# The end of the last expert in another order: a decoder trunk on one core

## The chip, the cores and the metric

The kernel runs on one core of a Trainium2 chip. The metric is the device time of one execution in microseconds (us); the runs shown are three executions. The engines are called by the names of the profile: PE is TensorE (matrix products), PEld its weight loads, DVE is VectorE, ACT is ScalarE, POOL is GpSimd, SP is SyncE, which here issues all transfers.

## The reference, cut to what matters

Two decoder layers over 256 tokens of width 1024. The part around the change is the end of the second layer: eight experts, each token sent to two of them, then a layer norm, then a gate with the input embedding.

```python
def moe(x, w_r, w1, w3, w2):                       # x: 256 tokens x 1024
    ...
    for e in range(N_EXPERTS):                     # 8 experts, inner width 3584
        out = out + combine[:, e:e + 1] * swiglu(xt, w1[e], w3[e], w2[e])

f = moe(x, ...)
x = layer_norm(DN_ALPHA * x + f, ln2_g[i], ln2_b[i])
gate = jax.nn.sigmoid(x @ ple_w_g[i] + ple_b_g[i])  # 1024 x 1024 weight
x = x + gate * (p[i] @ ple_w_p[i])
```

## The kernel before

The 256 tokens are two blocks of 128 rows (b = 0 and 1). Weights come through one stream of 1 MB loads ("raw" tiles, `Stream.load`, L204) that SP issues in a fixed order, up to eight in flight. The buffers are ten ring tiles and nine "cut" slots which the stream may borrow while the experts run.

Experts (`moe`, L1056): each expert has four steps of columns; a step is an up product (tiles `m`), SiLU and product on ACT and DVE (`mh`), a transposition on PE (`mt`, L1150) and a down product into the tile `py`. Expert weights are used as plain f32. When an expert is done, `rows` (L1161) copies its result out of PSUM as a high part (ACT, L1169) and a rest (DVE, L1170), tile `y`, and `spread` (L1180) multiplies it by the routing matrix on PE (tile `sc`, L1192), once for each block and each half of 512 columns; DVE adds it with its weight to the accumulator `acc` (L1193). For the first seven experts `spread` runs one expert later, between weight loads; for the eighth nothing comes after it.

The end (`finish`, L875, one generator for each block): layer norm of `acc[b]` on DVE (BN_STATS, BN_AGGR, L437 `n_w`, an inverse root on POOL L439 `n_r`, then L520 and L521, two instructions each, into `xn`); eight transpositions on PE (L455, `x2T_t`), whose results ACT and DVE write as a high part and a rest (L443, `x2T`); then `product` (L468): the gate weight comes in four 1 MB loads = eight pieces of 128 rows; each piece is split into a high part by ACT (L159) and a rest, the "second part", by DVE (L161), tile `hl`; a piece costs six matmuls of 512 columns into two PSUM banks `fin` (L462 high x high, L464 x the weight's rest, L466 the rest of x). So a block costs 48 matmuls. The two blocks use the same split pieces; `side_by_side` (L237) lets block 1 follow block 0 by up to six pieces (`LAG_G`). At the product's start the bias goes in as a one-row matmul for each bank (L472). `gated` (L806) does the sigmoid on ACT, two DVE operations and the store of each bank.

Each engine runs its own instructions strictly in the order written in its queue; that order is fixed when the program is built, by a scheduler that takes the program's order and the priorities (`high_priority`), and an instruction that waits holds all behind it on its engine.

Of the kernel before, what the change touches and what calls it, by code (L numbers as in the profile page):

```python
# [15 lines left out]
OP = mybir.AluOpType  # L16
# [51 lines left out]
TAFT = 4  # L68
STEPS = (2, 4)
# [35 lines left out]
class Stream:  # L105
# [3 lines left out]
    def __init__(self, tc, nc, raw, cut):  # L109
        self.tc = tc  # L110
        self.nc, self.rings, self.cut = nc, [raw], cut
        self.idle, self.busy, self.lend, self.lent = list(range(SPL)), {}, 0, []
        self.extra = []
        self.room, self.size = [RAW], [RAW]
        self.units, self.pieces, self.lags, self.stays = [], [], [], set()
        self.left = [None]
# [8 lines left out]
        self.whole, self.held = set(), {}  # L125
# [11 lines left out]
    def _split(self, v):  # L137
# [40 lines left out]
    def add_ring(self, pool, n):  # L178
        self.rings.append(pool)
        self.room.append(n)  # L180
        self.size.append(n)
        self.left.append(None)

    def raw_tile(self, name, stays=False, dtype=F32):

        for r in range(len(self.rings)):
            if self.room[r] and self.left[r] != 0:
                self.room[r] -= 1
                if self.left[r] is not None:
                    self.left[r] -= 1  # L190
                elif stays:
                    self.left[r] = self.size[r] - 1
# [56 lines left out]
def trunk(ctx: ExitStack, tc: tile.TileContext, a, out):  # L249
# [57 lines left out]
    for i in range(DEPTH):  # L307
# [15 lines left out]
        else:  # L323
# [144 lines left out]
    def product(b, ps, xT, ks, between=iter(()), bias=None):  # L468

        if bias is not None:  # L470
            for c in range(2):
                nc.tensor.matmul(ps[c], lhsT=one, rhs=bias[:, c * 512:(c + 1) * 512], start=True, stop=False)  # L472
        held = []
        for n, k in enumerate(ks):
# [391 lines left out]
    moe(tc, a, st, x, acc, xtp, rt, early, ident, const, small, ps_mm, ps_tr, ps_s, mm3, split_from)  # L866
    st.alone = False
    st.lend = 0
    late = ctx.enter_context(tc.tile_pool(name="late", bufs=2))
    st.load()  # L870
    row, pbg = st.raws[rows0], st.raws[rows0 + 1]
    rows_bc[f"L{last}g2"], rows_bc[f"L{last}b2"] = row[:, :D], row[:, D:]
    xn = [late.tile([P, D], F32, name=f"xn{b}", bufs=1) for b in range(NB)]

    def finish(b):  # L875

        if b == 0:
            xT = [late.tile([P, KT, P], F32R, name=f"x2T{b}{j}", bufs=1) for j in range(2)]
        else:
            t, _ = st.raw_tile("x2T1", dtype=F32R)  # L880
            xT = [t[:, j * D:(j + 1) * D].rearrange("p (k t) -> p k t", k=KT) for j in range(2)]
        ps = [ps_mm(b, f"fin{b}{c}") for c in range(2)]
# [3 lines left out]
        if b == 0:  # L886
            st.limit = None
            st.after = [normed.ins] * TAFT
        yield from product(b, ps, xT, range(KT), bias=pbg[0:1, :D])
        gated(b, ps, L_[last]["pp"][b], xn[b])  # L890

    side_by_side(st, [finish(b) for b in range(NB)])
# [163 lines left out]
def moe(tc, a, st, x, acc, xtp, rt, early, ident, const, small, ps_mm, ps_tr, ps_s, mm3, split_from):  # L1056
# [5 lines left out]
    with tc.tile_pool(name="moe", bufs=2) as mp:  # L1062
# [98 lines left out]
        def rows(e, py):  # L1161
# [18 lines left out]
        def spread(e, y, plT):  # L1180
# [6 lines left out]
            for b in range(NB):  # L1187
# [20 lines left out]
        for s, (e, c) in enumerate(steps):  # L1208
            hh = up(s, xg)
# [133 lines left out]
```

## Time and profile before

| what | us |
|---|---|
| runs | 1299.16, 1298.37, 1297.72; median 1298.37 |
| the profiled execution, its own time | 1299.9 |
| its span (first to last instruction in the trace) | 1298.0 |
| busy: PE, PEld, DVE, ACT, POOL | 1239.5, 725.6, 424.0, 309.9, 26.7 |
| last expert weight has landed | 1249.95 |
| block 0's transpositions start | 1263.08 |
| block 1's transpositions start | 1277.17 |
| last gate matmul ends | 1290.6 |
| last DVE instruction ends, span ends | 1292.7, 1298.0 |

All times of the trace are counted from the span's start. The profiled execution took 1.9 us more than its span, and 1.5 us more than the median run. A matmul's row shows when it starts and how long it is in the engine; matmuls overlap, so the step from one start to the next is what one costs.

### The profile page before, as it was taken

How to read it: one execution, taken by the hardware profiler on the slowest of the kernel's cores; microseconds unless marked ns; L12 is line 12 of the kernel's file. 1: busy time of each engine (PE TensorE's matmuls, PEld its weight loads, DVE VectorE, ACT ScalarE, POOL GpSimd, SP SyncE). 2: the span in 40 equal slices, each digit the busy share in tenths (PEclk: the TensorE clock that was granted, in tenths of full speed). 3: DMA queues.
4: the chain of work that ended last, by engine and by line, in shares of the span. 5: the costliest groups of instructions: out<-in, count | busy, mean ns of one | idle time of the engine just before them, and what ended most of it. 6: DMA issues, size and time to landing. Idle time of an engine off the chain costs nothing.

```text
span 1298.0 us, 27799 instructions
## 1 busy us (share of the span) xinstructions
PE 1239.5 (95%) x12214; PEld 725.6 (56%) x12214; DVE 424.0 (33%) x772; ACT 309.9 (24%) x505; POOL 26.7 (2%) x71
## 2 busy tenths in 40 slices
PE   8999999999999999999999999999899999978787
PEld 7888888887888556533323555533455543312126
DVE  7868554558876121011010111011012112001035
ACT  6754443445663101010100100010000001000022
POOL 1100000000100000000000000000000000000000
PEclk9999999999999899999999999999999999999988
DMA  9626554656549999999999999999999999999970
GB/s 328 228 65 207 184 177 150 223 188 194 206 143 371 405 364 364 356 421 421 421 420 420 420 420 419 420 421 420 420 420 419 419 420 420 421 421 421 421 287 35
DMA packets 83406, 431.59 MB, mean 333 GB/s; under 512 B 8615, under 2 KB 15309, under 8 KB 40270
## 3 DMA queue, kind: packets, MB, share of 16 engines
q1 hardware_dynamic: 83278, 429.74, 83.5%
q8 instruction: 98, 1.61, 0.5%
q14 instruction: 30, 0.25, 0.1%
HBM read 428.66 MB, written 1.05 MB: 331 GB/s over the span
## 4 chain that ended last, share of the span: by engine, by line
PE 72%; DMA 24%; DVE 2%; ACT 1%; issue 1%; POOL 0%; SPq 0%; ACTq 0%
DMA raw<-in_moe_w 23%; PE m L1110 17%; PE py L1110 8%; PE m L1105 7%; PE ff L462 3%; PE ff L464 3%; PE ff L466 3%; PE py L1105 3%; PE f L466 2%; PE f L462 2%; PE f L464 2%; PE g L988 2%; PE mt L1150 1%; PE sc L1192 1%; PE fin L462 1%; PE fin L464 1%
## 5 line engine op out<-in xcount | busy, mean ns | idle before, releaser
L1105 PE MATMUL m<-raw,xg 128*32 128x512 f32 x2240 | 251.0, 594 | 15.1 <-DMA raw<-in_moe_w 14.4
L1110 PE MATMUL m<-raw,xg 128*32 128x256 f32 x3024 | 225.8, 381 | 2.2 <-DMA raw<-in_moe_w 1.4
L1111 PE MATMUL m<-raw,xg 128*32 128x256 f32 x1008 | 224.0, 381 | 0.0
L1110 PEld LDWEIGHTS m<-raw,xg 128*32 128x32 f32 x3024 | 129.6, 110 | 87.1 <-issue 4.3
L1105 PEld LDWEIGHTS m<-raw,xg 128*32 128x32 f32 x2240 | 68.8, 110 | 185.5 <-issue 140.9
L161 DVE TENSOR_TENSOR hl<-raw,hl 128x1024 fp32r<-128x1024 f32 (+2 forms) x111 | 129.6, 1172 | 77.9 <-ACT hl L159 77.9
L1130 ACT ACTIVATE mh<-m 64x512 f32<-64x512 f32 (+1 forms) x56 | 33.1, 591 | 457.2 <-PE m L1105 245.2
L1105 PE MATMUL py<-raw,mhT 128*32 128x512 f32 x1120 | 132.7, 597 | 7.7 <-DMA raw<-in_moe_w 6.2
L159 ACT ACTIVATE hl<-raw 128x1024 fp32r<-128x1024 f32 (+2 forms) x111 | 112.5, 1021 | 107.6 <-PE ff L466 54.9
L1132 DVE TENSOR_TENSOR mh<-mh,m 64x512 f32<-64x512 f32 x35 | 24.1, 690 | 324.2 <-ACT mh L1130 323.7
L1110 PE MATMUL py<-raw,mhT 128*32 128x256 f32 x1512 | 114.3, 380 | 0.0
L1111 PE MATMUL py<-raw,mhT 128*32 128x256 f32 x504 | 113.6, 380 | 0.0
L1111 PEld LDWEIGHTS m<-raw,xg 128*32 128x32 f32 x1008 | 109.5, 110 | 0.0
L1110 PEld LDWEIGHTS py<-raw,mhT 128*32 128x32 f32 x1512 | 60.5, 110 | 42.3 <-issue 0.9
L1134 DVE TENSOR_TENSOR mh<-mh,m 96x256 f32<-96x256 f32 x21 | 8.8, 418 | 218.3 <-ACT mh L1130 218.0
L1105 PEld LDWEIGHTS py<-raw,mhT 128*32 128x32 f32 x1120 | 31.4, 109 | 79.7 <-issue 59.1
L1081 ACT ACTIVATE mhT<-mt 128x512 f32<-128x512 f32 (+2 forms) x32 | 16.7, 521 | 235.3 <-PE py L1105 136.7
L462 PE MATMUL ff<-hl,L0x1T 128*128 128x512 f32 (+1 forms) x192 | 57.6, 377 | 0.1
L464 PE MATMUL ff<-hl,L0x1T 128*128 128x512 f32 (+1 forms) x192 | 57.2, 373 | 0.0
L466 PE MATMUL ff<-hl,L0x1T 128*128 128x512 f32 (+1 forms) x192 | 56.2, 372 | 0.0
L1111 PEld LDWEIGHTS py<-raw,mhT 128*32 128x32 f32 x504 | 53.5, 110 | 0.0
L1150 PEld LDWEIGHTS mt<-ident,mh 64*128 64x128 f32 (+1 forms) x224 | 19.2, 139 | 47.2 <-issue 24.1
(502 smaller groups left out, 1468.4 us busy)
## 6 DMA issues: line engine op xcount, KB each, us to landing
raw<-in_moe_w SPq DMA_DIRECT2D x336, 1024.0 KB, 19.8
raw<-in_ffn_w SPq DMA_DIRECT2D x40, 512.0 KB, 4.6
raw<-in_ffn_w SPq DMA_DIRECT2D x11, 1024.0 KB, 5.0
raw<-in_w_in SPq DMA_DIRECT2D x8, 1024.0 KB, 5.1
raw<-in_w_o SPq DMA_DIRECT2D x8, 1024.0 KB, 5.2
raw<-in_ple_w_g SPq DMA_DIRECT2D x8, 1024.0 KB, 4.8
raw<-in_w_in SPq DMA_DIRECT2D x4, 832.0 KB, 5.3
raw<-in_ple_w_p SPq DMA_DIRECT2D x2, 1024.0 KB, 7.0
```

The lines of the kernel that those rows point to most:

```text
L159: nc.scalar.activation(hi[:, :n], t[:, c0:c1], AF.Copy)
L161: nc.vector.tensor_tensor(lo[:, :n], t[:, c0:c1], hi[:, :n].bitcast(F32), op=OP.subtract)
L462: nc.tensor.matmul(o, lhsT=xh, rhs=w, start=start, stop=False)
L464: nc.tensor.matmul(o, lhsT=xh, rhs=w, start=False, stop=False)
L466: nc.tensor.matmul(o, lhsT=xl, rhs=w, start=False, stop=stop)
L988: nc.tensor.matmul(pg[k // n][:, k % n * S:(k % n + 1) * S], lhsT=x[b][:, k * P:(k + 1) * P], rhs=once, start=(b == 0 and k % n == 0), sto ...
L1105: nc.tensor.matmul(u[(2 * j + g) * G:(2 * j + g + 1) * G], lhsT=lhsT(g), rhs=w, start=start, stop=stop)
L1110: nc.tensor.matmul(main[g * G:(g + 1) * G], lhsT=lhsT(g), rhs=parts[j], start=start and j != 1, stop=stop, skip_group_check=True)
L1111: nc.tensor.matmul(side, lhsT=lhsT(j), rhs=wb[:, H2:], start=start and j != 1, stop=stop, skip_group_check=True)
L1130: nc.scalar.activation(h, uv[0][:S], AF.Silu)
L1132: nc.vector.tensor_tensor(h, h, uv[0][S:], op=OP.mult)
L1150: nc.tensor.transpose(banks[-1][:, q % m * S:(q % m + 1) * S], hh[:, q * P:(q + 1) * P], ident[:S, :S])
```

## The change

- The norm's gain and bias rows are loaded as single rows of 4 KB (before: spread over 128 partitions by the load, 512 KB each), and so is the gate's bias; the three loads are issued before the last expert's loads instead of after them. `early_rows` spreads the two norm rows over the partitions with four one-row matmuls and four ACT copies, while the last expert's second step runs. These units now live in borrowed cut slots, three of the nine, to the end.
- The bias matmuls (`bias`) are issued earlier: block 1's at the last expert's last step, block 0's between the last down products.
- `rows` writes both high parts first, then both rests (for the experts with two groups of columns).
- `spread` of the last expert is called block by block, from inside `finish`; block 1's comes when block 1's generator starts.
- `xn` and `x2T` live in stream tiles; the separate pool is gone. The two norm and transposition steps no longer have raised priority.
- The rests of pieces 3, 5 and 7 of the gate weight go to POOL instead of DVE.
- The last bank of block 1 is gated and stored in two halves of 256 columns.

```diff
+POOLED = (3, 5, 7)
...
-                nc.vector.tensor_tensor(lo[:, :n], t[:, c0:c1], hi[:, :n].bitcast(F32), op=OP.subtract)
+                (nc.gpsimd if v in self.pool else nc.vector).tensor_tensor(lo[:, :n], t[:, c0:c1], hi[:, :n].bitcast(F32), op=OP.subtract)
...
     def raw_tile(self, name, stays=False, dtype=F32):
+        if stays:
+            if len(self.lent) < self.lend and self.idle:
+                return self.lent_tile(name, dtype)
+            return None, None
...
             for s, (e, c) in enumerate(steps):
+                if s == len(steps) - len(WIDTHS):
+                    rows0 = len(st.units)
+                    st.add([(lambda t, j=j: t[0:1, j * D:(j + 1) * D], row(a[n][i])) for j, n in enumerate(("ln2_g", "ln2_b"))], [])
+                    st.add([(lambda t: t[0:1, :D], row(a["ple_b_g"][i]))], [])
+                    st.add([], [])
...
-            rows0 = len(st.units)
-            st.add([(lambda t, j=j: t[:, j * D:(j + 1) * D], spread(a[n][i], D)) for j, n in enumerate(("ln2_g", "ln2_b"))], [])
-            st.add([(lambda t: t[0:1, :D], a["ple_b_g"][i].rearrange("(o n) -> o n", o=1))], [])
+            gate0 = len(st.pieces)
...
+        cuts = [(0, 512), (512, 768), (768, 1024)] if b == 1 and xb is not x[b] else [(0, 512), (512, 1024)]
+        for c0, c1 in cuts:
+            s, q = slice(c0, c1), ps[c0 // 512][:, c0 % 512:c0 % 512 + c1 - c0]
+            nc.scalar.activation(q, q, AF.Sigmoid)
+            nc.vector.tensor_tensor(q, q, pp[:, s], op=OP.mult)
+            nc.vector.tensor_tensor(xb[:, s], xb[:, s], q, op=OP.add)
...
+    def early_rows():
+        at, to = st.raws[rows0], st.raws[rows0 + 2]
+        for n in range(4):
+            s = slice(n * 512, (n + 1) * 512)
+            ps = ps_tr(f"bc{n}")
+            nc.tensor.matmul(ps, lhsT=one, rhs=at[0:1, s], start=True, stop=True)
+            nc.scalar.activation(to[:, s], ps, AF.Copy)
...
-        with tc.high_priority(offset=BOOST):
-            normed = layer_norm_(f"n2{b}", acc[b], D, rows_bc[f"L{last}g2"], rows_bc[f"L{last}b2"], xn[b])
-            transposed(f"x2T{b}", xn[b], xT)
...
+        def finish(b):
+            t, _ = st.raw_tile(f"x2T{b}", dtype=F32R)
+            xT = [t[:, j * D:(j + 1) * D].rearrange("p (k t) -> p k t", k=KT) for j in range(2)]
+            spread_block(b)
+            if b == 0:
+                bias(0)
             normed = layer_norm_(f"n2{b}", acc[b], D, rows_bc[f"L{last}g2"], rows_bc[f"L{last}b2"], xn[b])
             transposed(f"x2T{b}", xn[b], xT)
...
+            yield from product(b, fin[b], xT, range(KT), begun=True)
+            gated(b, fin[b], L_[last]["pp"][b], xn[b])
...
-                for n in range(2):
-                    src, cs = py[0][n * S:(n + 1) * S], slice(n * CH, (n + 1) * CH)
+                for src, cs in parts:
                     nc.scalar.activation(y[:S, cs], src, AF.Copy)
+                for src, cs in parts:
                     nc.vector.tensor_tensor(y[S:, cs], src, y[:S, cs].bitcast(F32), op=OP.subtract)
...
         for s, (e, c) in enumerate(steps):
+            if s == len(steps) - 1:
+                bias(1)
...
             if c == 1 and e:
                 spread(e - 1, ys.pop(e - 1), plTs.pop(e - 1))
+                if e == NE - 1:
+                    early_rows()
         downs(len(steps) - 1)
-        spread(NE - 1, ys.pop(NE - 1), plTs.pop(NE - 1))
+        y, plT = ys.pop(NE - 1), plTs.pop(NE - 1)
+        finale(lambda b: spread(NE - 1, y, plT, (b,)))
```

Where the instructions stand. First PE of before, from the last down product to block 0's transpositions (`sc_10289` and `sc_10292` are block 0's halves of the last spread, `sc_10295` and `sc_10298` block 1's; `fin<-raw,one` is a bias matmul).

```order
3753 L1105 MATMUL py_9994<-raw_10090,mhT_10261 32x512 x8
3754 L1192 MATMUL sc_10289<-y_10284,plT_9905 128x512
3755 L472 MATMUL fin_10309<-raw_10184,one 128x512
3756 L1192 MATMUL sc_10292<-y_10284,plT_9905 128x512
3757 L1192 MATMUL sc_10295<-y_10284,plT_9905 128x512
3758 L472 MATMUL fin_10310<-raw_10184,one 128x512
3759 L1192 MATMUL sc_10298<-y_10284,plT_9905 128x512
3760 L472 MATMUL fin_10395<-raw_10184,one 128x512
3761 L472 MATMUL fin_10396<-raw_10184,one 128x512
3762 L455 MATMUL x2T_t_10324<-ident,xn_10305 128x128 x4
3763 L455 MATMUL x2T_t_10331<-ident,xn_10305 128x128 x4
3764 L462 MATMUL fin_10309<-hl_10340,x2T_10307 128x512
```

All four spreads and the four bias matmuls stand ahead of block 0's transpositions. Now PE of the changed kernel, in the middle of block 0's product (`hl_10363` is piece 4, `hl_10372` piece 5; `sc_10394` and `sc_10397` are block 1's spread, `x2T_t_10413` and `x2T_t_10420` block 1's transpositions, `fin_10314` and `fin_10315` block 0's banks).

```order
3794 L474 MATMUL fin_10314<-hl_10363,x2T_10307 128x512
3795 L474 MATMUL fin_10315<-hl_10363,x2T_10307 128x512
3796 L1216 MATMUL sc_10394<-y_10301,plT_9905 128x512
3797 L1216 MATMUL sc_10397<-y_10301,plT_9905 128x512
3798 L470 MATMUL fin_10314<-hl_10372,x2T_10307 128x512
3799 L472 MATMUL fin_10314<-hl_10372,x2T_10307 128x512
3800 L474 MATMUL fin_10314<-hl_10372,x2T_10307 128x512
3801 L470 MATMUL fin_10315<-hl_10372,x2T_10307 128x512
3802 L472 MATMUL fin_10315<-hl_10372,x2T_10307 128x512
3803 L474 MATMUL fin_10315<-hl_10372,x2T_10307 128x512
3804 L463 MATMUL x2T_t_10413<-ident,xn 128x128 x4
3805 L463 MATMUL x2T_t_10420<-ident,xn 128x128 x4
```

Block 1's spread has moved behind the thirtieth matmul of block 0, and only the six of piece 5 stand between it and block 1's transpositions; in before 44 matmuls of block 0 stood ahead of those. Pieces 6 and 7 of block 0 come after them, behind the twelve matmuls of block 1's pieces 0 and 1, since their two slots are those of pieces 0 and 1.

POOL of before and then of the changed kernel, the end of its queue (`n_r` is the inverse root of a block's norm; `hl_10354`, `hl_10372`, `hl_10442` are pieces 3, 5 and 7).

```order
38 L439 TENSOR_TENSOR L1ra_r<-L1ra_w,mhalf 128x1
39 L439 TENSOR_TENSOR L1n_r<-L1n_w,mhalf 128x1 x2
40 L439 TENSOR_TENSOR n_r<-n_w,mhalf 128x1 x2
```

```order
39 L447 TENSOR_TENSOR L1n_r<-L1n_w,mhalf 128x1 x2
40 L447 TENSOR_TENSOR n_r<-n_w,mhalf 128x1
41 L162 TENSOR_TENSOR hl_10354<-raw_10157,hl_10354 128x1024
42 L162 TENSOR_TENSOR hl_10372<-raw_10167,hl_10372 128x1024
43 L447 TENSOR_TENSOR n_r<-n_w,mhalf 128x1
44 L162 TENSOR_TENSOR hl_10442<-raw_10177,hl_10442 128x1024
```

Two of POOL's new subtractions stand right behind block 0's inverse root. DVE of the changed kernel, over the same stretch (it has `xn`, both SBUF inputs, and then the rests of pieces 0, 1, 2 and 4, before block 1's accumulation).

```order
685 L526 SCALAR_TENSOR_TENSOR xn<-xn,n_r,raw_9598 128x512 x2
686 L162 TENSOR_TENSOR hl_10345<-raw_10142,hl_10345 128x1024
687 L162 TENSOR_TENSOR hl_10348<-raw_10142,hl_10348 128x1024
688 L451 TENSOR_TENSOR x2T_10307<-x2T_t_10331,x2T_10307 128x512
689 L451 TENSOR_TENSOR x2T_10307<-x2T_t_10338,x2T_10307 128x512
690 L162 TENSOR_TENSOR hl_10351<-raw_10157,hl_10351 128x1024
691 L162 TENSOR_TENSOR hl_10363<-raw_10167,hl_10363 128x1024
692 L1217 SCALAR_TENSOR_TENSOR acc<-sc_10394,combs,acc 128x512
693 L1217 SCALAR_TENSOR_TENSOR acc<-sc_10397,combs,acc 128x512
```

In before DVE took block 1's accumulation ahead of block 0's norm, and block 1's norm stood among the splits of the pieces.

## Rows read from the trace of the kernel before

**Rows 1.** The page, chain that ended last, shares by engine.
```profile
PE 72%; DMA 24%; DVE 2%; ACT 1%; issue 1%; POOL 0%; SPq 0%; ACTq 0%
```

**Rows 2.** Windows: length, busy time (and count) by engine, PEclk, DMA share, GB/s.
```profile
1205.00:1250.00 45.00, 35.73 (x300) 8.72 (x301) 2.07 (x3) 2.75 (x5) 0.00 (x0) 1.00 0.98 404
...
1263.00:1277.00 14.00, 14.00 (x53) 11.22 (x53) 14.00 (x18) 5.22 (x6) 0.92 (x1) 0.78 0.01 1
```

**Rows 3.** Timeline, last down product to block 0's product: start, duration, engine, line.
```profile
1250.00 1.92 PE L1105 MATMUL py<-raw,mhT 128*32 128x512 f32 x16 [0.46 <-DMA raw<-in_moe_w]
1251.99 0.59 ACT L1169 ACTIVATE y<-py 64x512 fp32r<-64x512 f32 x1 [4.52 <-PE py L1105]
1252.61 0.68 DVE L1170 TENSOR_TENSOR y<-py,y 64x512 fp32r<-64x512 f32 x1 [14.17 <-ACT y L1169]
1253.33 0.60 ACT L1169 ACTIVATE y<-py 64x512 fp32r<-64x512 f32 x1 [0.75 <-DVE y L1170]
...
1255.24 2.00 ACT L159 ACTIVATE hl<-raw 128x1024 fp32r<-128x1024 f32 x2 [1.31 <-DMA raw<-in_ple_w_g]
...
1256.32 1.41 DVE L1193 SCALAR_TENSOR_TENSOR acc<-sc,combs,acc 128x512 f32<-128x512 f32 x2 [0.23 <-PE sc L1192]
...
1257.65 0.68 DVE L514 BATCH_NORM_STATS2 n_s<-acc 128x6 f32<-128x512 f32 x1
...
1260.14 0.20 DVE L516 BATCH_NORM_AGGREGATE n_mv<-n_s 128x2 f32<-128x12 f32 x1
...
1260.81 0.14 DVE L437 TENSOR_SCALAR n_w<-n_mv 128x1 f32<-128x1 f32 x1
...
1263.08 1.97 PE L455 MATMUL x2T_t<-ident,xn 128*128 128x128 f32 x8
...
1264.93 1.22 PE L462 MATMUL fin<-hl,x2T 128*128 128x512 f32 x2
```

**Rows 4.** The chain in order of time, pairs of gate matmuls: start, share taken.
```profile
1267.00 0.85 PE fin L466 x2
...
1272.66 0.47 PE fin L462 x2
```

**Rows 5.** Windows of 1 us, the two falls of the clock (columns as in rows 2).
```profile
424.00:425.00 1.00, 0.00 (x0) 0.00 (x0) 0.88 (x7) 0.20 (x1) 0.00 (x0) 1.00 1.04 434
...
426.00:427.00 1.00, 0.94 (x4) 0.94 (x5) 0.78 (x6) 0.00 (x0) 0.00 (x0) 0.51 1.02 426
...
432.00:433.00 1.00, 1.00 (x19) 0.45 (x15) 0.00 (x0) 0.00 (x0) 0.00 (x0) 0.58 1.02 426
...
1255.00:1256.00 1.00, 0.48 (x1) 0.50 (x2) 0.97 (x2) 0.76 (x1) 0.00 (x0) 0.72 0.51 209
...
1269.00:1270.00 1.00, 1.00 (x6) 0.83 (x5) 1.00 (x2) 0.58 (x1) 0.00 (x0) 0.95 0.00 0
```

**Rows 6.** Timeline in layer 0, DVE and a POOL operation of 128x1024.
```profile
26.58 0.17 DVE L593 TENSOR_TENSOR L0kro<-L0kr 128x16 f32<-128x16 f32 x1
26.67 1.22 DVE L161 TENSOR_TENSOR hl<-raw,hl 128x1024 fp32r<-128x1024 f32 x1
27.16 1.71 POOL L613 TENSOR_SCALAR_AFFINE_SELECT L0ws<-L0ws 128x1024 f32<-128x1024 f32 x1 [4.61 <-DMA L0ws<-in_sg_w_s]
27.80 1.10 DVE L594 TENSOR_TENSOR L0kro<-L0kr 128x16 f32<-128x16 f32 x1
```

**Rows 7.** Timeline of PE, block 1's transpositions and first gate matmul.
```profile
1277.17 1.03 PE L455 MATMUL x2T_t<-ident,xn 128*128 128x128 f32 x8
1278.45 0.50 PE L462 MATMUL fin<-hl,x2T 128*128 128x512 f32 x1 [0.25 <-ACT x2T L443]
```

**Rows 8.** Timeline's last DVE row; DMA issues: count, KB each, us to landing.
```profile
1292.01 0.69 DVE L812 TENSOR_TENSOR xn<-xn,fin 128x512 f32<-128x512 f32 x1
...
raw<-in_moe_w SPq DMA_DIRECT2D x336, 1024.0 KB, 19.8
...
out<-xn SPq DMA_DIRECT2D x4, 256.0 KB, 2.6
```

More of the change, by code (lines that the diff above doesn't have):

```diff
@@ L115, in __init__ @@
         self.units, self.pieces, self.lags, self.stays = [], [], [], set()
-        self.left = [None]
         self.raws, self.ring, self.tiles = {}, {}, {}
@@ L124, in __init__ @@
         self.highs, self.lows = [], []
-        self.whole, self.held = set(), {}
+        self.whole, self.held, self.pool = set(), {}, set()
     def add(self, srcs, cuts, gains=None, lag=1):
@@ L181, in add_ring @@
         self.size.append(n)
-        self.left.append(None)
     def raw_tile(self, name, stays=False, dtype=F32):
+        if stays:
+            if len(self.lent) < self.lend and self.idle:
+                return self.lent_tile(name, dtype)
+            return None, None
         for r in range(len(self.rings)):
-            if self.room[r] and self.left[r] != 0:
+            if self.room[r]:
                 self.room[r] -= 1
[L189 to L192, printed above, removed]
                 return self.rings[r].tile([P, 2048], dtype, tag="raw", name=name), r
-        if stays:
-            return None, None
         if len(self.lent) < self.lend and self.idle:
-            slot = self.idle.pop(0)
-            self.lent.append(slot)
-            return self.cut.tile([P, 2048], dtype, tag=f"cut{slot}", name=name), ("cut", slot)
+            return self.lent_tile(name, dtype)
         if self.extra:
@@ L202, in raw_tile, with lent_tile @@
         return None, None
+    def lent_tile(self, name, dtype=F32):
+        slot = self.idle.pop(0)
+        self.lent.append(slot)
+        return self.cut.tile([P, 2048], dtype, tag=f"cut{slot}", name=name), ("cut", slot)
     def load(self, end=None):
@@ L283, in spread, with row @@
         return v.rearrange("(o n) -> o n", o=1).to_broadcast([P, n])
+    def row(v):
+        return v.rearrange("(o n) -> o n", o=1)
     def rows2(w, k0, cols):
@@ L466, in mm3, with product @@
             nc.tensor.matmul(o, lhsT=xl, rhs=w, start=False, stop=stop)
[L468 to L472, printed above, removed]
+    def product(b, ps, xT, ks, between=iter(()), begun=False):
         held = []
@@ L478, in product @@
             held.append((xk, hi, lo))
-            if bias is not None and len(ks) - COLS <= n < len(ks) - 1:
+            if begun and len(ks) - COLS <= n < len(ks) - 1:
                 continue
@@ L483, in product @@
                     mm3([ps[c] for c in cs], *xk, [hi[:, c * 512:(c + 1) * 512] for c in cs], [lo[:, c * 512:(c + 1) * 512] for c in cs],
-                        n == 0 and bias is None, n == len(ks) - 1 and m == len(held) - 1)
+                        n == 0 and not begun, n == len(ks) - 1 and m == len(held) - 1)
             held = []
@@ L864, in trunk @@
     last = DEPTH - 1
[L866 to L880, printed above, removed]
+    st.pool = {gate0 + j for j in POOLED}
@@ new lines, in trunk, with bias @@
+    fin, xn = [[], []], []
+    def bias(b):
+        fin[b] = [ps_mm(b, f"fin{b}{c}") for c in range(2)]
+        for c in range(2):
+            nc.tensor.matmul(fin[b][c], lhsT=one, rhs=st.raws[rows0 + 1][0:1, c * 512:(c + 1) * 512], start=True, stop=False)
+    def early_rows():
[5 more added lines that the diff above has]
+            nc.scalar.activation(to[:, s], ps, AF.Copy)
+        rows_bc[f"L{last}g2"], rows_bc[f"L{last}b2"] = to[:, :D], to[:, D:]
@@ L881, in finish, with finale @@
+    def finale(spread_block):
+        st.alone = False
+        st.load()
+        t, _ = st.raw_tile("xn")
+        xn.extend(t[:, b * D:(b + 1) * D] for b in range(NB))
+        def finish(b):
+            t, _ = st.raw_tile(f"x2T{b}", dtype=F32R)
             xT = [t[:, j * D:(j + 1) * D].rearrange("p (k t) -> p k t", k=KT) for j in range(2)]
-        ps = [ps_mm(b, f"fin{b}{c}") for c in range(2)]
-        with tc.high_priority(offset=BOOST):
+            spread_block(b)
+            if b == 0:
+                bias(0)
@@ L884, in finish @@
             normed = layer_norm_(f"n2{b}", acc[b], D, rows_bc[f"L{last}g2"], rows_bc[f"L{last}b2"], xn[b])
             transposed(f"x2T{b}", xn[b], xT)
[L886 to L892, printed above, removed]
+            if b == 0:
+                st.limit = None
+                st.after = [normed.ins] * TAFT
@@ L894, in redo @@
+            yield from product(b, fin[b], xT, range(KT), begun=True)
+            gated(b, fin[b], L_[last]["pp"][b], xn[b])
+        side_by_side(st, [finish(b) for b in range(NB)])
+    moe(tc, a, st, x, acc, xtp, rt, early, ident, const, small, ps_mm, ps_tr, ps_s, mm3, split_from, early_rows, bias, finale)
+    pbg = st.raws[rows0 + 1]
     def redo(w):
@@ L1053, in router_weights, with moe @@
     rt["expert"] = expert
-def moe(tc, a, st, x, acc, xtp, rt, early, ident, const, small, ps_mm, ps_tr, ps_s, mm3, split_from):
+def moe(tc, a, st, x, acc, xtp, rt, early, ident, const, small, ps_mm, ps_tr, ps_s, mm3, split_from, early_rows, bias, finale):
     nc = tc.nc
@@ L1166, in rows @@
                 y = mp.tile([P, D], F32R, tag="y", name=f"y{e}", bufs=1)
-                for n in range(2):
-                    src, cs = py[0][n * S:(n + 1) * S], slice(n * CH, (n + 1) * CH)
+                parts = [(py[0][n * S:(n + 1) * S], slice(n * CH, (n + 1) * CH)) for n in range(2)]
+                for src, cs in parts:
                     nc.scalar.activation(y[:S, cs], src, AF.Copy)
+                for src, cs in parts:
                     nc.vector.tensor_tensor(y[S:, cs], src, y[:S, cs].bitcast(F32), op=OP.subtract)
@@ L1178, in rows, with spread @@
             return hi, lo
-        def spread(e, y, plT):
+        def spread(e, y, plT, blocks=range(NB)):
             if not acc:
@@ L1186, in spread @@
                     nc.scalar.activation(acc[b], x[b], AF.Copy, scale=ALPHA)
-            for b in range(NB):
+            for b in blocks:
                 for n in range(2):
```

5 lines of the change are left out of this document (removed).

## The prediction

> **What bounds the kernel now.** I read the page's chain first, then windows by stage, then the timeline of the end. The chain is PE 72% and DMA 24% [rows 1]. While the experts run, the transfers are full (0.98 of their time) and PE is busy for 35.7 of 45 us [rows 2], so what is put on PE there has room. After the last expert weight three stretches follow. From 1250 to 1263 nothing is full: it is a chain of small steps from the last down product to block 0's transpositions, which start at 1263.08 [rows 3]. From there PE is dense to the last gate matmul, and in the first part DVE is full too: 14.00 of 14 us in 1263 to 1277 [rows 2]. The last 7.4 us are gate, store and landing. Only these stretches can move.
>
> PE's clock is half of that story. PE idles after the last down product, and the granted clock falls in the window at 1255 (0.72) and is back at 2.4 GHz in that at 1269 (0.95) [rows 5]; a pair of gate matmuls costs 0.85 us at 1.2 GHz and 0.47 at 2.4 [rows 4], 0.19 more for each matmul. From the first gate matmul (1264.93) to the recovery are some 4.0 us [rows 3, 5].
>
> **The change, step by step.** I work on the trace's times, then carry the difference to the median: the profiled execution took 1299.9, 1.9 more than its span.
>
> *Loads and early matmuls: 0.* The two 512 KB row loads become 4 KB loads and move ahead of the last expert on SP's queue. Eight loads of 19.8 us are in flight [rows 8], 2.5 us each; ten rings and six slots still hold sixteen, so the lost slots should not starve them. The gate weight comes 1 MB earlier; it was not late (its first split began at 1255.24, its first use is at 1264.93 [rows 3]). The eight one-row matmuls and four ACT copies fall where PE has 9.3 of 45 us free [rows 2]. Were that cover gone, eight at the slow step of one matmul (0.43, twice that at most) would cost 3 to 7 us.
>
> *Start of block 0: -3.4.* The second high part waited 0.75 us for DVE [rows 3]; now the two copies end at about 1253.1, the rests (0.68 each) at 1254.4, the two accumulations (1.41) at 1255.85, two BN_STATS of 0.68 at 1257.2, BN_AGGR 0.20 later. From n_w to the transpositions before took 1263.08 - 1260.81 = 2.27 [rows 3]. So they start at 1259.7. What falls out is block 1's accumulation and the bias matmuls between. Bounds -2.6 (one wait of 0.75 stays) to -3.9.
>
> *POOL's pieces 3 and 5: +4.0.* POOL takes them right behind n_r, while DVE still has xn and the rests of pieces 0 and 1, all with two inputs in SBUF. Rows 6 show what happens: the POOL operation was there at 27.16, ran only when DVE's subtraction ended (27.84), and DVE's next, 128x16, took 1.10 us instead of 0.17, to 28.9. The two take turns, and the POOL operation that waits goes first; it held DVE for 1.03 us with one input. Two inputs are not shown; from 1.0 (the same) to 3.4 (twice the whole 1.71) I take twice 1.03, 2.06, the hold being the nearest measure. Then piece 3's rest holds 1258.9 to 1260.95, half of xn follows, piece 5's rest holds to 1263.7, then the other half, rests 0 and 1 (1.22 each [rows 6]), and the x2T rest which piece 0's fifth matmul needs: 1267.4. Without POOL it would be there at 1263.2 and PE at 1263.3. Block 0's thirtieth matmul ends at 1274.4 instead of 1270.4 (4.9 matmuls at the slow step, 21.1 at 0.234 either way). Bounds 0 (no contention) to +6.6 (two holds of 3.4).
>
> The Trainium skill says of this pair of ports (SBUF — State Buffer, "Specifications (TRN2)") that VectorE with two SBUF inputs and GpSimd hold it exclusively, for a whole instruction. Rows 6 agree with 1.03 us; a sharing of bandwidth would have left a 128x16 instruction nearly as short as it was, and the sum near the first rival's. By the skill's figure for a two-input fp32 operation (GPSIMD Engine Reference, "3.1 Elementwise — side-by-side cycle accounting", 2.6 cycles for an element at 1.2 GHz) a hold would be an estimated 2.2 us, and the sum 0.4 more; no run here shows it.
>
> *Block 1's spread behind block 0's thirtieth matmul: +4.2.* In the new order the sum for block 1 (spread, two accumulations, statistics, xn) starts only there. From the first spread matmul to the transpositions: 0.4 (one matmul, inside the 0.47 of rows 4), two accumulations 1.41, two BN_STATS 1.36, BN_AGGR 0.20, and 2.27 from n_w on [rows 3] = 5.6 us, DVE by then idle. PE has piece 5 to cover it, 6 x 0.234 = 1.4; the spread's own two are 0.5 of the 5.6. So PE works 0.5 more and stands still for 3.7. Before, this norm lay under 44 matmuls and PE never waited for it. Bounds: 3.2 to 4.9.
>
> *The clock falls a second time: +2.4.* PE did nothing in the window at 424 and was down to 0.51 in that at 426 [rows 5]; after the down product (over at 1251.92 [rows 3]) it had only spread and bias matmuls and was falling at 1255. A stand of 3.7 us is longer than the one at 424. Then block 1's transpositions and first product take 1.85 us to the first gate matmul, as block 0's (1263.08 to 1264.93 [rows 3]), not 1.28 (1277.17 to 1278.45 [rows 7]): +0.57; and 4.0 us of matmuls at the slow step are 9.4 x 0.19 = +1.8. Bounds: 0 if the clock holds, +3.6 if it stays down as from 426 to 432.6 [rows 5], 6.6 us.
>
> *Pieces 6 and 7 of block 0: +0.9.* Three of nine slots are taken, so these two pieces are split only when block 1 has read pieces 0 and 1: ACT 1.0 [rows 3], then POOL 2.06, with the hand-overs about 3.2 us after the slot is free. PE has ten matmuls to fill 2.35 of it, all the rest of block 1 queued behind. Bounds 0 (POOL 1.0) to 2.2 (3.4).
>
> *The end: -0.4.* One bank in halves: the chain was a sigmoid and two DVE operations of 512 columns (0.69 each [rows 8]) and becomes a sigmoid and four of 256, of which the second sigmoid waits for the first half's product. I cost this at nothing. The last store is 128 KB instead of 256, which landed after 2.6 us [rows 8]; between +0.3 (one issue more) and -1.3 (half the landing) I take -0.4.
>
> Sum: -3.4 + 4.0 + 4.2 + 2.4 + 0.9 - 0.4 = +7.7 us. On the span that is 1305.7; on the median 1298.37 + 7.7 = **1306.1**.
>
> **Rivals.**
> *No contention.* POOL's pieces slip into DVE's gaps; the rest stays: -3.4 + 4.2 + 2.4 + 0.9 - 0.4 = +3.7, 1302.1. For it: only one 128x1024 POOL operation is shown in rows 6, with one input. Against: a 128x16 DVE operation held up sixfold.
> *The clock holds* while PE waits for block 1 (the wait is shorter, or the fall comes only after it): 7.7 - 2.4 = +5.3, 1303.7. With no contention as well, +1.3, 1299.7: about no change.
> *Faster: block 1's norm is hidden as before.* DVE was full from 1263 to 1277 and loses three rests of 1.2 us, so block 1's xn could be ready when PE gets there; then the 3.4 us at the start and 0.4 at the end stay: 1294.6. It decides from the point where PE waits under about 1 us for block 1's transpositions. For it: DVE's full row in rows 2. Against: the chain of 5.6 us begins at a PE instruction that stands six matmuls ahead of its user, whatever DVE's load.
>
> **Chances.** Forecast (contention and second fall) 0.50; no contention 0.18; clock holds 0.15; neither 0.07; faster 0.10. A measurement here tells 0.2%, 2.6 us, from no change: slower means above 1301.0. The forecast, the held clock, and three quarters of "no contention" are slower: 0.77. "Neither" and the rest of "no contention" are the same: 0.13. Faster 0.10. The range leaves out the faster case and the tail above two long holds: 1299.2 to 1309.2.
>
> **What would show it.** In the profile after: block 0's transpositions start before 1263, their second half held back by a POOL row of about 2 us, and a DVE row of xn or of a split two to three times its length beside it; a wait of PE of 3 to 4 us at block 1's transpositions, released by DVE; a second stretch of 0.50 in PEclk after 1276; a PE wait released by POOL at piece 7. Wrong would be: DVE rows of usual length beside POOL's; block 1's transpositions without a wait of PE; the last weight landing later than 1250.5, which would put the loss into the loads, where I have none.

## The result and the profile after

The changed kernel takes **1307.3 us** (median of 4 runs, 1306.4 to 1307.8) against 1298.7 for the kernel before in the same comparison (four runs: the three listed above and one more): 0.7% slower, ratio 1.0069, interval [1.0057, 1.0082]. The forecast was 1306.1, its range 1299.2 to 1309.2. The profiled execution took 1306.4, its span is 1304.7.

A span also carries what chance did earlier: PE's clock came back from its idle at 424 us almost 3 us sooner in this execution (0.98 in the window at 430, where before had 0.50, and 0.58 still at 432), in a part that did not change, and the last down product ends at 1249.9 instead of 1251.9. So I count from that end (the start of the last `py<-` row plus its length), in this and every later kernel: 46.1 us to the end of the span before, **54.8** after.

The timeline of the changed kernel, its start of block 0 (L447 is the inverse root, L525 and L526 are `xn`, L162 is a rest; compare [rows 3]):

```profile
1251.20 1.41 DVE L1194 TENSOR_TENSOR y<-py,y 64x512 fp32r<-64x512 f32 x2 [13.01 <-ACT y L1192]
...
1255.78 0.15 DVE L445 TENSOR_SCALAR n_w<-n_mv 128x1 f32<-128x1 f32 x1
1256.08 0.54 POOL L447 TENSOR_TENSOR n_r<-n_w,mhalf 128x1 f32<-128x1 f32 x1 [839.43 <-DVE n_w L445]
1256.15 3.50 DVE L525 SCALAR_TENSOR_TENSOR xn<-acc,n_mv,raw 128x512 f32<-128x512 f32 x2 [0.22 <-DMA raw<-in_ple_w_g]
1256.58 5.27 POOL L162 TENSOR_TENSOR hl<-raw,hl 128x1024 fp32r<-128x1024 f32 x2
1259.58 3.48 DVE L526 SCALAR_TENSOR_TENSOR xn<-xn,n_r,raw 128x512 f32<-128x512 f32 x2
1262.45 1.97 PE L463 MATMUL x2T_t<-ident,xn 128*128 128x128 f32 x8 [8.93 <-DVE xn L526]
```

The norm's sum is ready early (`n_w` 5.9 us after the down product, 8.9 before), and then POOL's two subtractions lie beside DVE's `xn`: each pair of `xn` rows takes 3.5 us. The transpositions start 12.5 us after the down product, 11.2 before. In the kernel before, the same two pairs took 1.41 (its timeline):

```profile
1260.87 1.41 DVE L520 SCALAR_TENSOR_TENSOR xn<-acc,n_mv,raw 128x512 f32<-128x512 f32 x2
...
1262.19 1.41 DVE L521 SCALAR_TENSOR_TENSOR xn<-xn,n_r,raw 128x512 f32<-128x512 f32 x2
```

PE around block 1's spread and transpositions, in the changed kernel:

```profile
1272.18 0.62 PE L1216 MATMUL sc<-y,plT 128*128 128x512 f32 x2
...
1273.78 0.39 PE L474 MATMUL fin<-hl,x2T 128*128 128x512 f32 x1
1277.68 1.97 PE L463 MATMUL x2T_t<-ident,xn 128*128 128x128 f32 x8 [3.51 <-DVE xn L526]
1279.48 1.22 PE L470 MATMUL fin<-hl,x2T 128*128 128x512 f32 x2
```

PE stands still for 3.51 us where it did not wait before [rows 7]. Windows of the changed kernel (columns as in [rows 2]; the sixth figure after the length is the granted clock):

```profile
1205.00:1250.00 45.00, 43.48 (x355) 12.05 (x354) 2.07 (x3) 2.78 (x6) 0.00 (x0) 0.96 1.02 419
1274.20:1277.70 3.50, 0.02 (x1) 0.02 (x1) 3.43 (x8) 0.00 (x0) 0.92 (x1) 0.84 0.00 0
1276.00:1277.00 1.00, 0.00 (x0) 0.00 (x0) 1.00 (x3) 0.00 (x0) 0.70 (x1) 0.77 0.00 0
1277.00:1283.00 6.00, 5.32 (x16) 4.38 (x17) 2.67 (x4) 1.75 (x3) 0.00 (x0) 0.50 0.00 0
```

After the stand TensorE is at 1.2 GHz from 1277 to 1283 (0.50): the second fall of the clock near the end. Then piece 7, and the end of the span (timeline, changed kernel):

```profile
1285.48 2.37 POOL L162 TENSOR_TENSOR hl<-raw,hl 128x1024 fp32r<-128x1024 f32 x1 [8.78 <-ACT hl L160]
1287.90 0.50 PE L472 MATMUL fin<-hl,x2T 128*128 128x512 f32 x1 [1.31 <-POOLq L1259]
...
1296.41 0.39 PE L474 MATMUL fin<-hl,x2T 128*128 128x512 f32 x1
1296.84 0.37 ACT L816 ACTIVATE fin<-fin 128x256 f32<-128x256 f32 x1 [1.46 <-PE fin L474]
...
1297.71 0.42 DVE L818 TENSOR_TENSOR xn<-xn,fin 128x256 f32<-128x256 f32 x1
1298.16 0.37 ACT L816 ACTIVATE fin<-fin 128x256 f32<-128x256 f32 x1 [0.95 <-DVE xn L818]
...
1299.03 0.42 DVE L818 TENSOR_TENSOR xn<-xn,fin 128x256 f32<-128x256 f32 x1
```

PE waits 1.31 us for piece 7's rest. The second half's sigmoid waits for the first half's *last* DVE step, so the two halves don't overlap: from the last matmul's end (1296.80) to DVE's end are 2.65 us, before 2.08.

### The profile page after: what moved, and what is told of

It reads as the page before. It is cut to its first block, busy times and chain, and to the rows that moved or that the text cites. A ratio compares the mean times of both kernels' runs of the same rounds, so it can differ in the third digit from the quotient of the medians.

```text
span 1304.7 us, 27836 instructions
## 1 busy us (share of the span) xinstructions
PE 1241.1 (95%) x12222; PEld 726.3 (56%) x12222; DVE 425.6 (33%) x771; ACT 312.8 (24%) x510; POOL 34.0 (3%) x74
## 5 line engine op out<-in xcount | busy, mean ns | idle before, releaser
L162 DVE TENSOR_TENSOR hl<-raw,hl 128x1024 fp32r<-128x1024 f32 (+2 forms) x108 | 126.1, 1172 | 80.5 <-ACT hl L160 80.4
L1155 DVE TENSOR_TENSOR mh<-mh,m 64x512 f32<-64x512 f32 x35 | 24.1, 690 | 326.6 <-ACT mh L1153 326.1
```

Of the source, the lines that this page charges most:

```text
L162: (nc.gpsimd if v in self.pool else nc.vector).tensor_tensor(lo[:, :n], t[:, c0:c1], hi[:, :n].bitcast(F32), op=OP.subtract)
L1155: nc.vector.tensor_tensor(h, h, uv[0][S:], op=OP.mult)
```

## The experiments

The theory: three separate losses, which together outweigh the 3 us gained at the start, namely POOL's contention with the norm, the place of block 1's spread, and the clock's fall in the gap that it makes. "End" is the time from the last down product to the end of the span; starts are counted from there too; both are read in one profiled execution of each kernel. Each ratio is to the kernel before in the same comparison, whose median was 1298.7 for experiments 1 to 4, 1298.1 for 5 to 8 and 1298.5 for 9 and 10.

| kernel | median us | ratio to before, interval | block 0's transpositions | block 1's | end |
|---|---|---|---|---|---|
| before | 1298.7 | | 11.2 | 25.3 | 46.1 |
| changed | 1307.3 | 1.0069 [1.0057, 1.0082] | 12.5 | 27.8 | 54.8 |
| 1 no POOL | 1301.6 | 1.0023 [1.0014, 1.0033] | 8.1 | 24.1 | 48.5 |
| 2 early spread | 1301.1 | 1.0016 [1.0007, 1.0025] | 11.6 | 22.8 | 48.3 |
| 3 both | 1296.8 | 0.9988 [0.9978, 0.9997] | 8.8 | 20.9 | 44.1 |
| 4 PE kept busy in the gap | 1305.3 | 1.0052 [1.0038, 1.0066] | 12.6 | 27.6 | 52.8 |
| 5 both, whole last bank | 1296.6 | 0.9988 [0.9979, 0.9997] | 9.1 | 21.2 | 44.0 |
| 6 as 5, PE kept busy at the start | 1296.0 | 0.9982 [0.9973, 0.9991] | 8.8 | 20.9 | 43.9 |
| 7 one-row matmuls thrice | 1316.8 | 1.0139 [1.0123, 1.0154] | 12.3 | 27.4 | 53.6 |
| 8 before, two rests on POOL | 1300.6 | 1.0015 [1.0006, 1.0024] | 13.2 | 26.8 | 48.4 |
| 9 as 6, block 1's norm first | 1296.5 | 0.9987 [0.9978, 0.9996] | 8.8 | 18.6 | 43.8 |
| 10 as 6, two rests less | 1295.3 | 0.9974 [0.9964, 0.9984] | 8.8 | 19.0 | 42.2 |

**1. No rest on POOL.**

```diff
-POOLED = (3, 5, 7)
+POOLED = ()
```

> The changed kernel with all second parts of the gate weight on VectorE again; all else stays. My theory: POOL's pieces 3 and 5 held the ports against DVE while block 0's norm was under way (its DVE rows L525 and L526 took 3.50 and 3.48 us, usual 1.41), worth 4.1 us, and piece 7 cost PE a wait of 1.31 us, of which about 0.5 goes. DVE's two further rests of 1.2 us come behind the norm and lie under PE's product. So 1307.3 - 4.6 = about 1302.7, block 0's transpositions start about 3 us earlier after the last down product, and the wait of 3.5 us at block 1's transpositions stays. Rival, no contention (the long rows of DVE are due to something else): within 1 us of 1307.3, since the rests only change engines.

Measured 1301.6, 5.7 less. The same two pairs of `xn` rows, in this kernel's timeline:

```profile
1256.40 1.41 DVE L525 SCALAR_TENSOR_TENSOR xn<-acc,n_mv,raw 128x512 f32<-128x512 f32 x2 [0.22 <-issue]
1257.73 1.41 DVE L526 SCALAR_TENSOR_TENSOR xn<-xn,n_r,raw 128x512 f32<-128x512 f32 x2
1258.53 1.97 PE L463 MATMUL x2T_t<-ident,xn 128*128 128x128 f32 x8 [4.80 <-DVE xn L526]
```

1.41 instead of 3.5: the contention is shown, 4.4 us at block 0's start, where I had expected about 3. The wait of 3.51 us at block 1 is still there, as expected. That 1.1 us more came back than I expected fits piece 7 (its whole wait goes) and a slow stretch after the second fall that is shorter in this profile.

**2. Block 1's spread beside block 0's.**

```diff
-            spread_block(b)
             if b == 0:
+                spread_block(0)
+                spread_block(1)
                 bias(0)
-            normed = layer_norm_(...)
-            transposed(...)
+            with tc.high_priority(offset=BOOST):
+                normed = layer_norm_(...)
+                transposed(...)
```

> The changed kernel with block 1's spread beside block 0's, as in the kernel before, and the raised priority of the norm; POOL keeps pieces 3, 5 and 7. My theory: block 1's sum then lies under block 0's matmuls, PE's wait of 3.5 us at block 1's transpositions goes, and with it the second fall of the clock, worth 2.4; block 1's two accumulations come into the way of block 0's norm, 1.4 back. So 1307.3 - 4.5 = about 1302.8, with no 0.50 in the clock after 1276. Rival, the wait comes from DVE's load and not from the place of the spread: a wait of 2 us or more stays and the time is above 1305.

Measured 1301.1, 6.2 less, 1.7 more than expected. PE reaches block 1's transpositions without a wait and at 2.4 GHz (PE's timeline, then one window of this kernel):

```profile
1274.27 0.39 PE L472 MATMUL fin<-hl,x2T 128*128 128x512 f32 x1
1274.50 0.60 PE L463 MATMUL x2T_t<-ident,xn 128*128 128x128 f32 x4
```

```profile
1274.00:1278.00 4.00, 3.98 (x22) 3.14 (x22) 1.36 (x2) 1.72 (x3) 0.00 (x0) 1.00 0.00 0
```

It was the place of the spread, not DVE's load. The edit raises the norm's priority too, and no run has the one without the other; but in the changed kernel block 1's transpositions start 5.5 us after its spread (1272.18 to 1277.68), which is the 5.6 that the prediction added up for an idle DVE, and DVE had stood idle for 3.80 us before its first accumulation. Another priority had nothing to shorten there. I had put the two accumulations at +1.4 on block 0's start; the start came 1.0 earlier instead, because POOL now took piece 3 mostly while DVE accumulated (more on this at the end).

**3. Both.** The two edits together.

> Both edits at once: no second part on POOL, and block 1's spread beside block 0's with the raised priority. My theory, the two losses are separate and add: 1307.3 - 4.6 - 4.5 = 1298.2, within 1.5 us of the kernel before. Rival, they overlap (POOL's delay of block 0 also shifts what block 1 waits for, so that one edit takes most of both): 1301 to 1303.

Measured 1296.8, 10.5 less than the changed kernel, a little below the kernel before. The sum of the single gains is 11.9, so 1.4 overlap. The second slow stretch accounts for 1.2 of it: the first twelve gate matmuls of block 1 are through 6.5 us after its transpositions start in the changed kernel, 5.3 in experiment 1 and 4.2 here, so the first edit's profile had part of it back already. Whether that edit or chance did this is not shown: in experiment 7, with POOL's rests and the same wait of 3.51 us, it is 5.8. Otherwise the two losses are separate.

**4. PE kept busy in the gap.** 17 matmuls into an unused bank, between block 1's spread and piece 5:

```diff
+            if b == 1:
+                idle_ps = ps_s("idle")
+                h = st.tiles[max(st.tiles)][0]
+                for n in range(17):
+                    nc.tensor.matmul(idle_ps, lhsT=x2Ts[0][0][:, n % KT, :], rhs=h[:, :512], ...)
...
```

> The changed kernel with 17 matmuls of 512 columns more on PE (into a bank that nobody reads) between block 1's spread and piece 5, so that PE has work where it stood still for 3.5 us. They end before block 1's norm does, so they delay nothing but block 0's piece 5, which is not urgent. My theory, the second fall of the clock costs 2.4 us by itself: block 1's transpositions start as in the changed kernel, but at 2.4 GHz, and the time is 1307.3 - 2.4 = about 1304.9. Rival, the clock falls anyway or its fall costs nothing: 1307.3, or more if the matmuls are in the way.

Measured 1305.3, 2.0 less. PE's timeline and the window behind the former gap:

```profile
1273.36 4.03 PE L908 MATMUL idle<-hl,x2T 128*128 128x512 f32 x17
...
1278.41 0.66 PE L463 MATMUL x2T_t<-ident,xn 128*128 128x128 f32 x4
```

```profile
1278.00:1282.00 4.00, 3.98 (x22) 2.97 (x21) 2.38 (x4) 1.75 (x3) 0.00 (x0) 1.00 0.00 0
```

Block 1's transpositions start when they did (27.6 against 27.8), the clock stays at 1.00, and the end is 2.0 shorter. The intervals of the two medians overlap, so it is the profiles that show this: the second fall is a loss of its own.

**5. The last bank whole again**, on top of experiment 3:

```diff
-        cuts = [(0, 512), (512, 768), (768, 1024)] if b == 1 and ... else [(0, 512), (512, 1024)]
+        cuts = [(0, 512), (512, 1024)]
```

> The kernel with both edits (no POOL, early spread; 1296.8) and the last bank gated and stored whole again, as before. My theory: the halves made the end longer, because the second half's sigmoid waited 0.95 us for the first half's last VectorE step (last matmul to end of span 7.9 us, against 7.4 in the kernel before); so 0.5 less, 1296.3. Rival, the prediction's own term (the smaller last store is worth 0.4): 1297.2. The time can hardly tell these; the stretch from the last matmul to the end of the span can.

1296.6: the time can't tell, as foreseen. The timeline of the end can:

```profile
1286.77 0.58 ACT L816 ACTIVATE fin<-fin 128x512 f32<-128x512 f32 x1 [1.46 <-PE fin L474]
...
1287.38 0.70 DVE L817 TENSOR_TENSOR fin<-fin,L1ppv 128x512 f32<-128x512 f32 x1 [0.62 <-ACT fin L816]
1288.12 0.69 DVE L818 TENSOR_TENSOR xn<-xn,fin 128x512 f32<-128x512 f32 x1
```

From the last matmul's end (1286.73) DVE ends after 2.08 us and the span after 7.4; in experiment 3, with halves, after 2.64 and 7.8. The halves cost 0.4 to 0.5 us. (In the changed kernel the two stores of 128 KB landed after a median of 2.2 us and the three of 256 KB after 2.1: the smaller size bought nothing.)

**6. PE kept busy at the start too**, on top of experiment 5:

```diff
                 spread_block(0)
                 spread_block(1)
+                keep_on()
...
+        keep_on(14, seen[0].ins, plT.rearrange("p b s -> p (b s)"))
-        finale(lambda b: spread(NE - 1, y, plT, (b,)))
+        finale(lambda b: spread(NE - 1, y, plT, (b,)), lambda: keep_on(16, seen[0].ins, y[0][:, :CH]))
```

(`seen[0]` is the last matmul written before: first the last down product's, then the last spread's.)

> As the kernel with both edits and the whole last bank, with 30 matmuls more on PE whose results nobody reads: 14 of 256 columns behind the last down product, and 16 of 512 behind block 1's spread, where PE waits for block 0's norm. My theory: they keep TensorE at 2.4 GHz, so that the first fall of the clock goes too; it costs 0.6 us at the transpositions and 1.8 us of slow matmuls. So about 1296.3 - 2.4 = 1293.9. Rival, the clock falls in spite of them: then 16 matmuls take 7 us, not 3.7, block 0's transpositions wait some 2.5 us for them and the time is about 1299.

Measured 1296.0, only 0.6 less, which the runs can't tell from nothing, and the end no shorter (43.9 against 44.0). Yet the clock did what I said: it stays at 1.00 (windows of this kernel, first to block 0's transpositions, then to block 1's), and PE waits for DVE instead (its timeline):

```profile
1252.00:1260.00 8.00, 6.67 (x30) 4.49 (x28) 7.90 (x14) 5.91 (x7) 0.91 (x1) 1.00 0.33 133
1260.00:1271.60 11.60, 10.09 (x42) 6.80 (x41) 11.60 (x17) 1.20 (x2) 0.92 (x1) 1.00 0.00 0
```

```profile
1255.28 3.81 PE L1261 MATMUL idle<-y,plT 128*128 128x512 f32 x16
1259.56 1.32 PE L463 MATMUL x2T_t<-ident,xn 128*128 128x128 f32 x8 [0.47 <-DVE xn L526]
...
1263.69 0.73 PE L472 MATMUL fin<-hl,x2T 128*128 128x512 f32 x2 [0.53 <-DVE hl L162]
...
1271.63 1.29 PE L463 MATMUL x2T_t<-ident,xn 128*128 128x128 f32 x8 [0.75 <-DVE xn L526]
```

DVE is full, 11.60 of 11.60 us. And PE had to wait for DVE already in experiment 5, where it was slow at the start (its timeline):

```profile
1271.28 1.29 PE L463 MATMUL x2T_t<-ident,xn 128*128 128x128 f32 x8 [0.76 <-DVE xn L526]
```

0.76 us there and 0.75 here: what PE won by its clock it spent in waiting. In this order the slow clock at the start was hidden behind DVE, which neither of my theories had.

**7. The one-row matmuls of `early_rows` three times.**

```diff
-            nc.tensor.matmul(ps, lhsT=one, rhs=at[0:1, s], start=True, stop=True)
+            for _ in range(3):
+                nc.tensor.matmul(ps, lhsT=one, rhs=at[0:1, s], start=True, stop=True)
```

> The changed kernel with each of the four one-row matmuls that spread the norm's rows issued three times: eight more. It tests the cover that the prediction gave the early matmuls (its term of 0). My theory: in the changed kernel PE has only 45 - 43.5 = 1.5 us free between 1205 and 1250, so little cover is left: eight more cost 3.4 us at least, of which 1.9 or more stands at the end: 1309.2 to 1312. Rival, PE is only busy because it is slow there, and catches up with the loads: 1307.3.

Measured 1316.8, 9.5 more than the changed kernel and far above my 1309.2 to 1312. All of it lies ahead of the last down product, which ends at 1263.8 (a row from 1260.14, 3.64 long): from the first expert's transposition `gt` (456.4) that is 807.4 us, 12.6 more than in the changed kernel. The end is 1.2 shorter in this execution; the second fall comes later in it (the granted clock is 1.00 through the whole stand and 0.50 from 1293 to 1296), so that block 1's eight transpositions take 1.32 us and not 1.97. First the changed kernel's PE timeline and one of its windows, then this one's timeline and windows:

```profile
1194.95 1.12 PE L887 MATMUL bc<-raw,one 1*128 1x512 f32 x2
...
1197.85 2.93 PE L887 MATMUL bc<-raw,one 1*128 1x512 f32 x6
```

```profile
1200.00:1208.00 8.00, 8.00 (x32) 1.60 (x34) 0.00 (x0) 1.06 (x2) 0.00 (x0) 0.59 1.01 422
```

```profile
1200.84 14.31 PE L888 MATMUL bc<-raw,one 1*128 1x512 f32 x20
```

```profile
1200.00:1215.00 15.00, 15.00 (x32) 5.23 (x21) 0.00 (x0) 2.39 (x4) 0.00 (x0) 0.63 1.01 422
1215.00:1220.00 5.00, 5.00 (x25) 1.19 (x28) 0.00 (x0) 0.60 (x1) 0.00 (x0) 0.50 1.01 421
```

A one-row f32 matmul is two rows of the trace, about 1.0 us (8 rows in 3.9 us). Here ten of them in a row (14.31 us) let the clock fall to 1.2 GHz, which slows the expert's work behind them as well (0.50 still in 1215 to 1220). The changed kernel has this fall too, behind its last three: 0.59 in 1200 to 1208, where the kernel before has 1.00. There it cost no time, but the cover was nearly used up: PE waits for no load any more between 1205 and 1250, where before it waited about half a microsecond for each of 1 MB.

**8. The kernel before, with the rests of pieces 3 and 5 on POOL and nothing else.**

```diff
-                nc.vector.tensor_tensor(lo[:, :n], t[:, c0:c1], ...)
+                (nc.gpsimd if v in self.pool else nc.vector).tensor_tensor(lo[:, :n], t[:, c0:c1], ...)
...
+    st.pool = {gate0 + j for j in (3, 5)}
```

> The kernel before, with nothing changed but the second parts of pieces 3 and 5, which go to POOL. My theory, the contention belongs to POOL's subtractions and not to the new order: VectorE's xn rows beside them become 3.5 us, block 0's transpositions start 3 to 4 us later, and the time is 1298.7 + 3.5 = 1302.2. Rival, POOL is harmless here and VectorE gains 2.4 us: 1298.7 or less.

Measured 1300.6, 2.5 more than before by the medians of this comparison; I had expected 3.5. Its timeline:

```profile
1261.36 1.40 DVE L522 SCALAR_TENSOR_TENSOR xn<-acc,n_mv,raw 128x512 f32<-128x512 f32 x2
...
1262.46 2.49 POOL L161 TENSOR_TENSOR hl<-raw,hl 128x1024 fp32r<-128x1024 f32 x1
1262.68 3.49 DVE L523 SCALAR_TENSOR_TENSOR xn<-xn,n_r,raw 128x512 f32<-128x512 f32 x2
...
1269.56 4.56 DVE L161 TENSOR_TENSOR hl<-raw,hl 128x1024 fp32r<-128x1024 f32 x2
```

One hold falls on the norm here (3.49 - 1.41 = 2.08), not two, since piece 5 comes later: it holds two rests of DVE (4.56 us, usual 2.35). Block 0 starts 2.0 later. POOL's loss doesn't need the new order.

**9. Block 1's norm ahead of the rests of pieces 4 and 5**, on top of experiment 6:

```diff
-            with tc.high_priority(offset=BOOST):
+            with tc.high_priority(offset=40 if b else BOOST):
```

> The kernel with the 30 further matmuls (1296.0), and block 1's norm one step higher in priority, so that VectorE computes it after the rests of pieces 0 to 3 and ahead of those of pieces 4 and 5. There the clock stayed at 2.4 GHz but PE waited three times for VectorE (0.53, 0.23, 0.75 us), so that 0.6 was gained and not 2.4. My theory: VectorE's order is now what holds PE; block 1's transpositions come up to 2.4 us earlier, and of this 0.5 to 1.5 us reach the end: about 1295.0. Rival, VectorE's load as a whole decides, whatever its order, since the rests of pieces 4 and 5 are then late for PE: 1296.0.

Measured 1296.5, near the rival's number and not to be told from experiment 6. Block 1's transpositions do start 2.3 us earlier (18.6), but PE lost 1.72 us to a rest just before (its timeline), and the end stays at 43.8:

```profile
1266.52 0.73 PE L472 MATMUL fin<-hl,x2T 128*128 128x512 f32 x2 [1.72 <-DVE hl L162]
```

**10. Two rests less**, on top of experiment 6:

```diff
-            with order:
+            if v in self.bare:
+                lo = hi
+            else:
+              with order:
...
+    st.bare = {gate0 + j for j in (3, 5)}
```

> The kernel with the 30 further matmuls (1296.0), with the rests of pieces 3 and 5 left out: their matmuls take the high part a second time (this part of the product is changed), so that PE has the same work and VectorE two subtractions of 1.2 us less. My theory: VectorE's load between the last down product and block 1's transpositions is what took the place of the slow clock; block 1's transpositions start up to 2.4 us earlier and the end by 1.5 to 2.4: 1293.6 to 1294.5. Rival, PE or the norm's chain is the bound there: 1296.0.

Measured 1295.3, 0.7 less than experiment 6; the intervals overlap, and it is less than the 1.5 that I set as the least. In the profiled execution the end is 1.7 shorter (42.2), block 1's transpositions start 1.9 earlier and wait for nothing, and from 1263 to 1271 PE is busy all 8 us (7.1 in experiment 6). So direction and place are as the theory had them, and the size is open. Together with experiment 9 this speaks for DVE's load, and not its order, as what stands behind PE there.

## Why the prediction was right, step by step

- *Loads and early matmuls, 0*: held. From the first expert's transposition `gt` (456.6 before, 455.1 after) to the last down product's end are 795.3 us before and 794.8 after. But the cover was thinner than the 9.3 us that I read: PE is busy for 43.5 of 45 us, 35.7 before [rows 2]. I had put a one-row matmul at 0.43 us, 0.87 at most; it costs 1.0 and can cost the clock besides (experiment 7).
- *Start of block 0, -3.4*: 3.0 (experiment 1: 8.1 against 11.2). I named block 1's accumulation among what falls out; in experiment 3 it is back beside block 0's, with the norm's priority raised, and 2.3 of the 3.0 stay. So most must come from the other edits (the order of the copies, the early bias matmuls), which no run separates.
- *POOL's pieces 3 and 5, +4.0*: 4.4 at the transpositions; at block 1's spread, behind the thirtieth matmul, it is 22.3 against 18.6 in experiment 1, 3.6. The mechanism held, and the hold is 2.08 for each piece. That I had 2.06 is luck: [rows 6] have no 27.84, the subtraction's row ends at 27.89 and DVE's next is 0.93 longer than usual, not 1.03, and the doubling for a second input was a choice between 1.0 and 3.4. I also had the second hold fall between the two halves of `xn`; both were over (POOL's two rows end at 1261.85) before the first half was ready. So the transpositions start 1.4 us later after the down product than before, and "before 1263" came true (1262.45) only because that product ended 2.0 earlier.
- *Block 1's spread, +4.2*: PE waits 3.51 (3.7 forecast) and does the spread's two matmuls; gone in experiment 2.
- *The second fall, +2.4*: 2.0 (experiment 4).
- *Pieces 6 and 7, +0.9*: 1.31.
- *The end, -0.4*: wrong in sign, +0.5. I let the second sigmoid follow the first half's product, and it followed the first half's add. This term was mis-sized by 0.9.

By these terms the sum is -3.0 + 3.6 + 4.0 + 2.0 + 1.3 + 0.5 = +8.4 against +8.7 measured from the down product on and +8.6 in the medians. The forecast of +7.7 is 0.9 short, the size of the end's error; the other terms are off by 0.2 to 0.4 in both directions and cancel, which is luck too. The rivals fall one by one: "no contention" by experiments 1 and 8, "the clock holds" by the window at 1277, "block 1's norm is hidden" by the 3.51 us. The chances were added up slightly wrong: by their own parts slower has 0.785 (not 0.77) and the same 0.115 (not 0.13).

The prediction had the early sum as a gain and the rest as losses. The experiments bear this out: without the losses the kernel is 0.1 to 0.2% faster than before (experiments 3, 5, 6). What it did not see is the fall of the clock behind the one-row matmuls, and that the slow clock at block 0's start cost almost nothing in an order where DVE is full (experiment 6).

## What to carry to other kernels

Work moved to an idle engine has to be priced by what it holds, not by what it saves: here a rest costs DVE 1.2 us, and on POOL it held DVE for 2.1. Work that starts a chain (here the spread that feeds a norm) should stand as far ahead of its user as the chain is long, and a gap on PE can cost twice, as the one of 3.51 us did here, by the wait and by the clock after it. Before a slow clock is repaired, look at who is full in that stretch: here DVE was, and the repaired clock gave almost nothing.

## What the runs showed of the hardware

In these kernels POOL's rests held DVE where DVE had two inputs in SBUF. In experiment 2 POOL's subtraction of piece 3 lies beside DVE's accumulations, which read one input from PSUM, and reaches into the first pair of `xn` rows (timeline, POOL and DVE):

```profile
1256.89 2.35 POOL L162 TENSOR_TENSOR hl<-raw,hl 128x1024 fp32r<-128x1024 f32 x1 [840.31 <-DMA raw<-in_ple_w_g]
1256.92 0.73 DVE L1219 SCALAR_TENSOR_TENSOR acc<-sc,combs,acc 128x512 f32<-128x512 f32 x1
...
1257.68 0.70 DVE L1219 SCALAR_TENSOR_TENSOR acc<-sc,combs,acc 128x512 f32<-128x512 f32 x1
...
1258.36 2.09 DVE L525 SCALAR_TENSOR_TENSOR xn<-acc,n_mv,raw 128x512 f32<-128x512 f32 x2
...
1260.15 2.49 POOL L162 TENSOR_TENSOR hl<-raw,hl 128x1024 fp32r<-128x1024 f32 x1
1260.37 3.48 DVE L526 SCALAR_TENSOR_TENSOR xn<-xn,n_r,raw 128x512 f32<-128x512 f32 x2
```

0.73 and 0.70 us are the usual length. The first `xn` pair starts while POOL still runs and takes 2.09 instead of 1.41; the second has a whole rest beside it and takes 3.48. So a rest on POOL was free beside the accumulation and dear beside the norm. The Trainium skill says the same (SBUF — State Buffer, "SBUF: two separate sides", where the rule that the prediction drew on stands): only a DVE operation in a two-port mode, or one with two SBUF inputs against a GpSimd operation that reads SBUF, contends with GpSimd. These rows agree for two SBUF inputs; no run here shows a two-port mode.
